# Six changes of queue order in a two-block fp32 transformer kernel: taps, key stacks, rotation tables, modulated tiles, key weights, and one root in SBUF

## The chip, the core and the metric

The kernel runs on one core of a Trainium2 chip. The metric is the device time in microseconds (us) of one execution; the median of several runs counts. The core has a matrix engine (PE), a vector engine (DVE), a scalar engine (ACT), a general engine (POOL, called G in the code), and SP, whose queue here issues the DMAs. Each engine works through its own queue in the order in which the program holds it; engines wait for one another by semaphores.

## The reference

Two transformer blocks are computed one after the other on 512 tokens of width 1024, all in fp32, batch 1. Cut to what matters:

```python
def first_block(x, ...):
    h = rms_norm(x, norm1_g)
    proj = h @ w_in                      # q, keys and values, u_conv, gates
    y_attn = nsa_attention(...) @ w_attn_br
    y_conv = conformer_conv(u_conv, ...) @ ...   # depthwise conv, 31 taps, 512 channels
    g_a, g_b = split(sigmoid(g_merge))
    x = x + (g_a * y_attn + g_b * y_conv) @ w_out
    x = x + conv_ffn(rms_norm(x, norm2_g), ffn_w_up, ..., ffn_w_down)
    return rms_norm(x, final_g)

def second_block(x, c, ...):
    # twice: h = rms_norm(x) * (1 + scale(c)) + shift(c); x = x + gate(c) * mixer(h)
    # mixer 1: dense attention with rotated q and k, and latent attention
    # mixer 2: windowed attention with sinks
    return rms_norm(x, final_norm)
```

## The kernel before

Activations lie transposed: eight tiles X[0] to X[7] (in the trace `x`) hold 128 features each by 512 tokens. A matrix product `gemm` sums over eight 128-feature tiles, and every fp32 operand is split in a high and a low part, so that one product is three PE matmuls (`mm3`: low times high, high times low, high times high; L133 to L135). A product of one 128x512 output tile over eight tiles is 24 matmuls.

A weight passes through `wload` (L101 to L114): SP issues a DMA into a raw buffer (`t` or `wr`), ACT copies the high part (L112, `wh`), and POOL or DVE subtracts to get the low part (L113, `wl`). Tiles `m`, `h`, `z` are the same parts where a weight goes to another pool. A raw buffer is free for the next DMA once the subtraction has read it; the buffers of a pool are used in turn. Which engine subtracts, and which raw pool is used, alternates by `wpools`. The order in which the four engines take their work comes from a scheduler that lays the program out ahead of time, from the order of the code and from `tc.issue_after`, which keeps an instruction from being placed ahead of a named one. Nothing is reordered at run time.

Output tiles collect in PSUM banks. Products with `wide_bank` go round the banks `pg` and `ps`, four in all; the next product in a bank waits until the engine that reads the last one (the eviction) is done.

The places that the change touches, in order of time:

- `stack_k` (L291) copies a key tile into 64-row halves: two ACT copies (L297, L299) and two DVE instructions. Four calls for the block keys `KB` stand ahead of the loop over `natural` (L478), whose four products are evicted by ACT (L488).
- `gates` makes the merge gates, each a product of 24 matmuls. The taps of convolution channel tile 0 are one ACT multiplication (L520) and one POOL addition (L521) each; those that are left over when the attention is done (`rest`, 16) are spread over the gates of the first call.
- The feed-forward down product runs in three passes. The last 128-feature tiles of weights are taken in two halves of 256 tokens by `by_halves`: eight output tiles for the first half, then eight for the second. After each half the sum of squares gives a norm: `newton` computes the inverse root by eleven small DVE instructions (L177 to L188) between SBUF and PSUM, `row_bcast` spreads it by PE (L204), and `modulated` makes eight normalised tiles (DVE L851, ACT L852, DVE L853). For the first half the eight tiles are made while PE works on the second. `by_halves` also serves the products `w_eo` and `w_oo`.
- After the first half of the down product the weights `w_kv` and `w_qa` are loaded. Then four small tables for the rotation of q and k are made by POOL (L908).
- In the `w_eo` product the squares are ACT instructions (L243, L246), summed by DVE (L254) and PE (L264). The weights `w_ok` of the keys that follow are loaded by the same `wload`.

## Time and profile before

| what | value |
|---|---|
| median of 3 runs | 1297.09 us (1296.65 to 1299.78) |
| profiled execution, its own time | 1301.25 us |
| span of the profiled execution | 1299.5 us |
| PE busy | 1251.2 us, 96% of the span |
| DVE, ACT, POOL busy | 68%, 54%, 56% |

The span is the time from the first to the last instruction of the profiled execution; what lies around it is 1.75 us here. Times in the text are microseconds from the span's start. In the rows, names are tiles of the program, `a<-b` reads "a is made from b", and `xN` is a count. The clock in the tables of stretches is the granted clock of PE as a share of full speed: 1.00 is 2.4 GHz, 0.50 is 1.2 GHz.

### The profile page before, as it was taken

The page shows a single profiled execution, that of the slowest core. Times are in us where ns is not written, and L with a number is a line of the kernel's source. Part 1 is how long each engine was busy: PE and PEld are TensorE (multiplying, and loading weights), DVE is VectorE, ACT ScalarE, POOL GpSimd, SP SyncE. Part 2 cuts the span into 40 slices and gives each one's busy share as a digit, 9 for nine tenths or more (in the row PEclk, how much of TensorE's full clock was granted, in tenths as well). Part 3 has the DMA queues.
Part 4 walks back from the last instruction along what each step waited for, and adds up shares of the span by engine and source line. Part 5 has one row for each costly group of instructions (what it writes and reads, how often), then busy time and mean ns, then how long its engine had stood idle before and what let it go on. Part 6 is the DMA issues. An engine that isn't in the chain of part 4 may idle for free. (4 is left out here: it accounts for less than half of the span.)

```text
span 1299.5 us, 19323 instructions
## 1 busy us (share of the span) xinstructions
PE 1251.2 (96%) x6369; PEld 1041.1 (80%) x6369; DVE 883.7 (68%) x2000; ACT 701.9 (54%) x1488; POOL 730.1 (56%) x718
## 2 busy tenths in 40 slices
PE   7999998999999999999999999999999989999997
PEld 6878876888888888888887798877777788888786
DVE  6756666986644878776777258576787766656565
ACT  6756777434444444423443243585766635766554
POOL 5557875773644666655665423386664423676542
PEclk9999998999999999999999999999999989999998
DMA  6221111342434555576553402111111111111221
GB/s 220 90 75 58 33 44 47 91 147 73 138 98 129 165 169 166 161 254 221 171 159 94 145 23 56 49 45 58 53 50 41 33 50 57 58 57 57 66 74 65
DMA packets 71971, 124.74 MB, mean 96 GB/s; under 512 B 8256, under 2 KB 17344, under 8 KB 71872
## 3 DMA queue, kind: packets, MB, share of 16 engines
q1 hardware_dynamic: 71872, 123.52, 30.8%
q8 instruction: 50, 0.82, 0.3%
q14 instruction: 49, 0.40, 0.1%
HBM read 121.39 MB, written 2.10 MB: 95 GB/s over the span
## 5 line engine op out<-in xcount | busy, mean ns | idle before, releaser
L113 POOL TENSOR_TENSOR wl<-wr,wh 128x512 fp32r<-128x512 f32 (+2 forms) x215 | 281.1, 1311 | 260.8 <-ACT wh L112 205.8
L133 PE MATMUL pg<-h,wl 128*128 128x512 f32 x628 | 250.2, 398 | 5.8 <-POOL wl L113 3.9
L135 PE MATMUL pg<-h,wh 128*128 128x512 f32 x628 | 248.0, 395 | 0.0
L134 PE MATMUL pg<-h,wh 128*128 128x512 f32 x628 | 247.6, 394 | 0.0
L112 ACT ACTIVATE wh<-wr 128x512 fp32r<-128x512 f32 (+2 forms) x215 | 132.6, 618 | 164.2 <-PE pg L135 77.7
L133 PEld LDWEIGHTS pg<-h,wl 128*128 128x128 f32 x628 | 119.1, 190 | 29.6 <-POOL wl L113 4.9
L135 PEld LDWEIGHTS pg<-h,wh 128*128 128x128 f32 x628 | 119.0, 189 | 23.3
L134 PEld LDWEIGHTS pg<-h,wh 128*128 128x128 f32 x628 | 119.1, 190 | 22.5 <-issue 0.7
L113 POOL TENSOR_TENSOR m<-t,m 128x512 fp32r<-128x512 f32 (+1 forms) x67 | 89.6, 1337 | 77.3 <-ACT m L112 73.4
L337 DVE TENSOR_TENSOR t<-pt,t 128x512 fp32r<-128x512 f32 (+1 forms) x160 | 97.5, 631 | 28.7 <-ACT t L336 27.4
L342 PE MATMUL po<-t,h 128*128 128x512 f32 (+3 forms) x384 | 110.7, 364 | 4.4 <-DVE t L337 1.9
L133 PE MATMUL ps<-h,wl 128*128 128x512 f32 x260 | 103.1, 396 | 3.2 <-POOL wl L113 3.2
L135 PE MATMUL ps<-h,wh 128*128 128x512 f32 x260 | 102.2, 393 | 0.0
L134 PE MATMUL ps<-h,wh 128*128 128x512 f32 x260 | 101.8, 391 | 0.0
L336 ACT ACTIVATE t<-pt 128x512 fp32r<-128x512 f32 (+1 forms) x160 | 84.3, 552 | 22.6 <-PE pt L332 21.9
L342 PEld LDWEIGHTS po<-t,h 128*128 128x128 f32 x384 | 65.7, 188 | 29.2 <-ACT t L336 13.7
L332 PE MATMUL pt<-k,p 128*128 128x128 f32 x576 | 85.3, 273 | 2.9 <-POOL p L1010 2.9
L332 PEld LDWEIGHTS pt<-k,p 128*128 128x128 f32 x576 | 69.0, 140 | 14.0 <-POOL p L1010 4.4
L1010 POOL TENSOR_SCALAR p<-p,s 128x512 f32<-128x512 f32 x64 | 45.4, 712 | 55.6 <-DVE s L1009 53.5
L778 DVE CUSTOM_DVE_ANT_0 b<-b,z 128x512 f32<-128x512 f32 x48 | 75.5, 1572 | 0.0
L112 ACT ACTIVATE m<-t 128x512 fp32r<-128x512 f32 (+2 forms) x76 | 46.2, 608 | 31.0 <-PE ps L133 9.4
L133 PEld LDWEIGHTS ps<-h,wl 128*128 128x128 f32 x260 | 49.1, 189 | 14.9 <-POOL wl L113 4.8
(441 smaller groups left out, 3046.1 us busy)
## 6 DMA issues: line engine op xcount, KB each, us to landing
b<-ada_t SPq DMA_DIRECT2D x48, 256.0 KB, 3.1
z<-ada_t SPq DMA_DIRECT2D x48, 256.0 KB, 3.2
t<-w_up SPq DMA_DIRECT2D x44, 256.0 KB, 2.9
wr<-w_up SPq DMA_DIRECT2D x44, 256.0 KB, 2.8
wr<-w_g SPq DMA_DIRECT2D x32, 256.0 KB, 2.9
t<-w_dn SPq DMA_DIRECT2D x23, 256.0 KB, 2.7
wr<-w_br SPq DMA_DIRECT2D x16, 256.0 KB, 2.6
wr<-w_gt SPq DMA_DIRECT2D x16, 256.0 KB, 2.9
```

The costliest lines, as they stand in the source:

```text
L112: A.activation(hi[:, :z], raw[:, :z], AF.Copy)
L113: eng.tensor_sub(lo[:, :z], raw[:, :z], f(hi[:, :z]))
L133: PE.matmul(ps, ll, rh, start=start and i == 0, stop=False)
L134: PE.matmul(ps, lh, rl, start=False, stop=False)
L135: PE.matmul(ps, lh, rh, start=False, stop=stop and i == n - 1)
L332: PE.transpose(ps[:, o:o + 128], src, ident)
L336: evac[:] = [A.activation(hi[:, :n], ps[:, :n], AF.Copy)]
L337: evac.append(V.tensor_sub(lo[:, :n], ps[:, :n], f(hi[:, :n])))
L342: PE.matmul(o[:, a:b], v, t[:, pa:pa + b - a], start=start and z == 0, stop=stop and z == 1)
L778: V.tensor_tensor_reduce(out=raw, in0=raw, in1=CA[z], op0=OP.mult, op1=OP.add, scale=1.0, scalar=0.0, accum_out=MA[l][:, z, m:m + 1])
L1010: scaled[0] = G.tensor_scalar(p, p, sm[:, 1:2], 0.0, op0=OP.mult, op1=OP.add)
```

## The change

Six edits. (A) The 16 left-over taps of tile 0 begin with the third gate: none in the first two, 16 over the other 12. (B) The key stacks move into the loop over `natural`, after its second and fourth product. (C) The rotation tables are kept behind the last POOL subtraction of a weight that stood in the program when the first half of the down product ended (`halved`). (D) The modulated tiles of the first half no longer stand ahead of the second half's evictions: each follows the eviction of the same number (`then`), in the down product and in `w_eo`. (E) The key weights `w_ok` are kept behind the last square of the first half of `w_eo`. (F) The two roots of `w_oo` use `newton_alone`: eight instructions, all in SBUF.

```diff
+        sub = eng.tensor_sub(lo[:, :z], raw[:, :z], f(hi[:, :z]))
+        if eng is G:
+            halved[:] = [sub]
...
+    def newton_alone(x):
+        n = x.shape[1]
+        y, t = [new("s", (128, 20))[:, :n] for _ in range(2)]
+        V.tensor_scalar(y.bitcast(I32), x.bitcast(I32), -0.5, float(0x5F3759DF), op0=OP.mult, op1=OP.add)
+        V.tensor_mul(t, y, y)
+        V.scalar_tensor_tensor(t, t, -0.5 * 0.375, x, op0=OP.mult, op1=OP.mult)
+        V.scalar_tensor_tensor(y, t, 1.5 * 0.375, y, op0=OP.add, op1=OP.mult)
+        V.tensor_mul(t, y, y)
+        V.scalar_tensor_tensor(t, t, 64.0 / 9, x, op0=OP.mult, op1=OP.mult)
+        V.scalar_tensor_tensor(t, t, -10.0 / 3, t, op0=OP.add, op1=OP.mult)
+        root[:] = [V.scalar_tensor_tensor(y, t, 5.0, y, op0=OP.add, op1=OP.mult)]
+        return y
...
-    for t in tkb:
-        KB.append([stack_k(t, 0), stack_k(t, 64)])
...
+        if i % 2:
+            KB.append([stack_k(tkb[i // 2], 0), stack_k(tkb[i // 2], 64)])
...
-            for t in rest[len(rest) * i // len(todo):len(rest) * (i + 1) // len(todo)]:
+            j, k = max(i - 2, 0), len(todo) - 2
+            for t in rest[len(rest) * j // k:len(rest) * (j + 1) // k] if i > 1 else ():
                 conv_tap(0, t)
...
-    def by_halves(src, k0, k1, xs, evac, raw, ws):
+    def by_halves(src, k0, k1, xs, evac, raw, ws, then=[]):
...
                     with after_root():
                         evac(th, m, ps[:, 0:256], c)
+                    if m < len(then):
+                        then[m]()
...
-        for k in range(KT):
-            modulated(k, fgn[:, k:k + 1], md[:, k:k + 1], R[:, 256:512], c)
+        then[:] = [lambda k=k, R=R, c=c: modulated(k, fgn[:, k:k + 1], md[:, k:k + 1], R[:, 256:512], c)
+                   for k in range(KT)]
+        for step in then if th else ():
+            step()
         xr.append((r0, c))
         if th == 0:
+            tables_after = halved[0]
...
+            with tc.issue_after(getattr(tables_after, "ins", tables_after)):
+                G.tensor_tensor(t, cc(tname).rearrange("p (i d) -> p i d", d=64),
+                                row[:, go:go + 64].unsqueeze(1).to_broadcast([128, 4, 64]), op=OP.mult)
...
+        if th == 0:
+            first_squared = squared[0]
...
-        ps = gemm(I["w_ok"][m], H)
+        with tc.issue_after(getattr(first_squared, "ins", first_squared)):
+            ps = gemm(I["w_ok"][m], H)
...
-        R = row_bcast(rsqrt(sums[th].sums("po"), 1.0 / D, EPS), "pt")
+        R = row_bcast(rsqrt(sums[th].sums("po"), 1.0 / D, EPS, alone=True), "pt")
```

How the instructions stand on the engines shows more than the diff. Line numbers of the changed kernel are higher by 1 to 32 (L113 is L114 there, L521 is L539, L246 is L264, L851 is L873, L908 is L935, L1156 is L1183).

POOL at the first merge gates, before: `h_1077` is the sum of the taps, and `wl_2808` and `wl_2814` are the two low weights of the second gate.

```order
L614 TENSOR_SCALAR p_2586<-p_2586,s_2618,k_521 128x512
L521 TENSOR_TENSOR h_1077<-h_1077,r_2661 128x512
L521 TENSOR_TENSOR h_1077<-h_1077,t_2803 128x512
L113 TENSOR_TENSOR wl_2808<-wr_2806,wh_2807 128x512
L113 TENSOR_TENSOR wl_2814<-wr_2812,wh_2813 128x512
L521 TENSOR_TENSOR h_1077<-h_1077,t_2851 128x512
```

The same in the changed kernel; the second gate's lows are now `wl_2805` and `wl_2811`, and the third gate's are `wl_2850` and `wl_2856`.

```order
L114 TENSOR_TENSOR wl_2766<-wr_2764,wh_2765 128x512
L114 TENSOR_TENSOR wl_2805<-wr_2803,wh_2804 128x512
L114 TENSOR_TENSOR wl_2811<-wr_2809,wh_2810 128x512
...
L632 TENSOR_SCALAR p_2586<-p_2586,s_2618,k_497 128x512
L539 TENSOR_TENSOR h_1077<-h_1077,r_2661 128x512
L114 TENSOR_TENSOR wl_2850<-wr_2848,wh_2849 128x512
L114 TENSOR_TENSOR wl_2856<-wr_2854,wh_2855 128x512
```

The second gate's lows moved from behind the first left-over tap to right behind the first gate's, 33 rows earlier in the queue.

POOL in the second pass of the down product, before: `wl_7376` to `wl_7470` are the low weights of its last four output tiles.

```order
L113 TENSOR_TENSOR wl_7347<-wr_7345,wh_7346 128x384
L113 TENSOR_TENSOR h_7665<-t_7663,h_7664 128x512
L113 TENSOR_TENSOR wl_7376<-t_7374,wh_7375 128x512
L113 TENSOR_TENSOR wl_7382<-wr_7380,wh_7381 128x384
L113 TENSOR_TENSOR wl_7411<-t_7409,wh_7410 128x512
L113 TENSOR_TENSOR wl_7417<-wr_7415,wh_7416 128x384
L113 TENSOR_TENSOR wl_7464<-wr_7462,wh_7463 128x512
L113 TENSOR_TENSOR wl_7470<-t_7468,wh_7469 128x384
```

The same in the changed kernel; `b` are the rotation tables, `h_7745` and `h_7757` low parts of `w_qa`.

```order
L114 TENSOR_TENSOR h_7665<-t_7663,h_7664 128x512
L935 TENSOR_TENSOR b_8038<-k_8036,k_108 128x256 x2
L935 TENSOR_TENSOR b_8041<-k_8036,k_108 128x256
L114 TENSOR_TENSOR wl_7376<-t_7374,wh_7375 128x512
L935 TENSOR_TENSOR b_8041<-k_8036,k_108 128x256
L114 TENSOR_TENSOR wl_7382<-wr_7380,wh_7381 128x384
L114 TENSOR_TENSOR wl_7411<-t_7409,wh_7410 128x512
L114 TENSOR_TENSOR wl_7417<-wr_7415,wh_7416 128x384
L114 TENSOR_TENSOR wl_7464<-wr_7462,wh_7463 128x512
L114 TENSOR_TENSOR h_7745<-t_7743,h_7744 128x512
L114 TENSOR_TENSOR h_7757<-t_7755,h_7756 128x512
L114 TENSOR_TENSOR wl_7470<-t_7468,wh_7469 128x384
```

The tables left two places further ahead (before `wl_7236` and before `wl_7277`) and now stand in front of `wl_7376` and `wl_7382`; two subtractions for `w_qa` now stand in front of `wl_7470`. ACT at the same place, in the changed kernel; before, `wh_7469` came right behind `wh_7463`:

```order
L113 ACTIVATE wh_7416<-wr_7415 128x384
L113 ACTIVATE wh_7463<-wr_7462 128x512
L113 ACTIVATE h_7738<-wr_7737 128x512
L113 ACTIVATE h_7744<-t_7743 128x512
L113 ACTIVATE h_7756<-t_7755 128x512
L113 ACTIVATE wh_7469<-t_7468 128x384
```

Three copies of `w_qa` weights moved ahead of `wh_7469`; the buffer `wr_7737` that the first of them reads is one that `wl_7417` has to free before its DMA is issued.

ACT at the end of the first half of `w_eo`, before; `p_11164` and `p_11188` are the squares of the last two X tiles, and `wh` are the key weights.

```order
L246 ACTIVATE p_11141<-x_114 128x256
L112 ACTIVATE wh_11596<-wr_11595 128x512
L246 ACTIVATE p_11164<-x_115 128x256
L112 ACTIVATE wh_11639<-wr_11638 128x512
L112 ACTIVATE wh_11645<-wr_11644 128x512
L246 ACTIVATE p_11188<-x_116 128x256
```

The same in the changed kernel.

```order
L264 ACTIVATE p_11141<-x_114 128x256
L264 ACTIVATE p_11164<-x_115 128x256
L264 ACTIVATE p_11188<-x_116 128x256
L113 ACTIVATE wh_11590<-wr_11589 128x512
L113 ACTIVATE wh_11596<-wr_11595 128x512
L113 ACTIVATE wh_11639<-wr_11638 128x512
```

The squares no longer stand behind weights. A little later DVE's sixteen modulation instructions (L851, L853), which stood ahead of the third eviction of the second half (`x_111`), are mixed with the evictions, one tile of each kind at a time.

## Rows read from the trace of the kernel before

**Rows 1.** The page's first line: busy us, share of the span, instructions.

```profile
PE 1251.2 (96%) x6369; PEld 1041.1 (80%) x6369; DVE 883.7 (68%) x2000; ACT 701.9 (54%) x1488; POOL 730.1 (56%) x718
```

**Rows 2.** PE's waits: line, what ended them, us in total, times, longest.

```profile
PE pg L133 <- POOL wl L113: 3.9, 2, 3.7
PE ps L133 <- POOL wl L113: 3.2, 4, 1.5
PE po L264 <- DVE z L254: 3.0, 2, 2.8
...
PE ps L133 <- DVE x L1156: 2.0, 1, 2.0
PE pg L133 <- ACT p L488: 1.9, 1, 1.9
```

**Rows 3.** Stretches: us, busy us of five engines, PE's clock, DMA share.

```profile
217.14:223.97 6.83, 5.92 (x14) 4.68 (x15) 2.45 (x4) 2.91 (x6) 6.83 (x6) 0.50 0.41 118
226.40:253.60 27.20, 27.20 (x122) 22.52 (x121) 24.55 (x37) 12.66 (x21) 19.18 (x15) 1.00 0.33 96
...
1046.58:1049.99 3.41, 3.41 (x18) 3.41 (x18) 0.97 (x7) 0.67 (x2) 2.22 (x2) 0.50 0.59 162
...
708.90:728.50 19.60, 16.28 (x67) 12.07 (x67) 8.37 (x13) 7.22 (x14) 14.90 (x13) 1.00 0.51 150
742.20:758.00 15.80, 15.80 (x126) 15.12 (x125) 3.64 (x8) 2.93 (x7) 0.00 (x0) 1.00 0.06 17
```

**Rows 4.** Timeline of POOL at the first gates: start, us, operation, idle before.

```profile
215.10 1.66 POOL L521 TENSOR_TENSOR h<-h,t 128x512 f32<-128x512 f32 x1 [10.62 <-ACT t L520]
216.72 2.52 POOL L113 TENSOR_TENSOR wl<-wr,wh 128x512 fp32r<-128x512 f32 x2
```

**Rows 5.** Timeline of ACT at the key stacks: the last copy, the first eviction.

```profile
47.89 0.63 ACT L299 ACTIVATE h<-p 64x512 fp32r<-64x512 f32 x1
48.54 0.49 ACT L488 ACTIVATE p<-ps,s 128x280 f32<-128x280 f32 x1
```

**Rows 6.** Timeline of POOL: the first rotation table alone, the last two.

```profile
696.05 0.74 POOL L908 TENSOR_TENSOR b<-k,k 128x256 f32<-128x256 f32 x1 [0.63 <-DVE p L789]
...
709.68 2.33 POOL L908 TENSOR_TENSOR b<-k,k 128x256 f32<-128x256 f32 x2
```

**Rows 7.** Timeline of POOL, second pass of the down product.

```profile
725.20 1.29 POOL L113 TENSOR_TENSOR h<-t,h 128x512 fp32r<-128x512 f32 x1
...
733.77 2.36 POOL L113 TENSOR_TENSOR wl<-wr,wh 128x384 fp32r<-128x384 f32 x2 [3.82 <-ACT wh L112]
```

**Rows 8.** DMA issues from 726 to 737: KB each, median us to landing.

```profile
wr<-w_kv SPq DMA_DIRECT2D x2, 256.0 KB, 3.7
wr<-w_qa SPq DMA_DIRECT2D x2, 256.0 KB, 3.5
```

**Rows 9.** Timeline of DVE in the same pass.

```profile
733.31 0.69 DVE L113 TENSOR_TENSOR m<-wr,m 128x512 fp32r<-128x512 f32 x1 [8.34 <-ACT m L112]
```

**Rows 10.** Timelines of DVE and ACT, end of the first half of `w_eo`.

```profile
1042.46 0.47 DVE L1156 SCALAR_TENSOR_TENSOR x<-ps,k,x 128x256 f32<-128x256 f32 x1
...
1044.35 0.63 ACT L112 ACTIVATE wh<-wr 128x512 fp32r<-128x512 f32 x1 [2.40 <-DMA wr<-w_ok]
```

**Rows 11.** Timeline of DVE over the two roots of `w_eo`.

```profile
1048.85 0.16 DVE L198 TENSOR_SCALAR s<-po 128x2 f32<-128x2 f32 x1 [2.72 <-PE po L264]
...
1052.62 1.26 DVE L851 SCALAR_TENSOR_TENSOR p<-x,k,pt 128x256 f32<-128x256 f32 x3 [0.76 <-PE pt L204]
...
1058.86 0.48 DVE L1156 SCALAR_TENSOR_TENSOR x<-ps,k,x 128x256 f32<-128x256 f32 x1
...
1071.36 1.07 DVE L853 SCALAR_TENSOR_TENSOR h<-p,k,h 128x256 fp32r<-128x256 f32 x2
```

**Rows 12.** Timeline of DVE at the last root: its first and last instruction.

```profile
1289.57 0.16 DVE L198 TENSOR_SCALAR s<-po 128x2 f32<-128x2 f32 x1 [1.15 <-PE po L264]
...
1291.63 0.16 DVE L188 SCALAR_TENSOR_TENSOR s<-po,s 128x2 f32<-128x2 f32 x1
```

More of the change, by code (lines that the diff above doesn't have):

```diff
@@ L194, in after_root, with rsqrt @@
         return tc.issue_after(getattr(root[0], "ins", root[0]))
-    def rsqrt(src, scale, eps, bank=None):
+    def rsqrt(src, scale, eps, bank=None, alone=False):
         x = new("s", (128, 20))[:, :src.shape[1]]
         V.tensor_scalar(x, src, scale, eps, op0=OP.mult, op1=OP.add)
-        return newton(x, bank)
+        return newton_alone(x) if alone else newton(x, bank)
     def row_bcast(col, tag="ps"):
@@ L879, in build @@
     xr = []
-    for th, c in by_halves(I["w_dn"], 18, 22, ACTV[18:], down, "t", ws):
+    then = []
+    for th, c in by_halves(I["w_dn"], 18, 22, ACTV[18:], down, "t", ws, then):
         v = new("s", (128, 16))[:, 0:4]
@@ L1159, in build @@
     H = [None] * KT
-    for th, c in by_halves(I["w_eo"], 4, 8, OC[4:], attn_out, "m", ws):
+    for th, c in by_halves(I["w_eo"], 4, 8, OC[4:], attn_out, "m", ws, then):
         R = row_bcast(rsqrt(sums[th].sums("po"), 1.0 / D, EPS), "pt")
-        for k in range(KT):
-            modulated(k, MOD[1][1][:, k:k + 1], MOD[1][0][:, k:k + 1], R[:, 0:256], c)
+        if th == 0:
+            first_squared = squared[0]
+        then[:] = [lambda k=k, R=R, c=c: modulated(k, MOD[1][1][:, k:k + 1], MOD[1][0][:, k:k + 1], R[:, 0:256], c)
+                   for k in range(KT)]
+        for step in then if th else ():
+            step()
     md = MOD[1][0]
```

8 lines of the change are left out of this document (4 added, 4 removed).

## The prediction

> **What bounds the kernel now.** I read the page's first line first, then PE's waits, then the granted clock by stretches, and last the timelines of the engines that end those waits. PE is busy for 96% of the span [rows 1], so the kernel can gain only where PE waits, or where it works at half clock; nothing else in the change has a price. The waits that the change aims at are five [rows 2]: 3.7 us for one POOL low weight at the merge gates, 3.2 us in four waits for lows in the down product, 2.8 us for a sum of squares `z`, 2.0 us for an eviction L1156, 1.9 us for an eviction L488. Some of them are followed by a stretch at a granted clock of 0.50, which is 1.2 of 2.4 GHz [rows 3]: 6.83 us after the 3.7 us wait, and 3.41 us after the 2.8 us wait (the row at 1046.58; two more of this length, at 49.89 and 1060.23, follow the waits of 1.9 and 2.0). Work at half clock takes twice as long, so these cost 5.92 / 2 = 3.0 us and 3.41 / 2 = 1.7 us. The waits in the down product lie in a stretch at 1.00 throughout [rows 3] (the row from 708.90): there only the waiting counts.
>
> Unit times: five gates of 24 matmuls take 27.20 us [rows 3], so a 512-wide matmul is 0.227 us and a gate 5.44; the 256-wide one of the halves is 0.12 (15.80 us by 126 records, the small sums among them).
>
> **A, taps.** POOL waits 10.62 us for the scaled input of a left-over tap, adds it, and only then makes the second gate's lows at 216.72 [rows 4]. In the changed order these lows stand right behind the first gate's, far ahead, and no tap stands before them. The wait (3.7) and the stretch at half clock (3.0) go: 6.7. The two subtractions (2.52) now come earlier on POOL among the attention's instructions, which may cost something there, and 16 taps in 12 gates mean two in some gates: 2.52 + 2 x 1.3 = 5.1 us of POOL against 5.44 of PE, which still fits. DVE, at 24.55 of 27.20 us in the gates [rows 3], has no part in these taps. I take 6.5, range 5 to 6.7.
>
> **B, key stacks.** Eight copies of some 0.63 stand on ACT ahead of the first L488 (48.54) [rows 5], and PE's bank waits for that eviction. Without them it runs when its product is done, and PE's 1.9 and the 1.7 of half clock go: 3.6. The copies (8 x 0.65 = 5.2 us of ACT) then stand between the later evictions, four behind the second and four behind the fourth; the third may be late. I take 3.2, range 2.2 to 3.6.
>
> **C, rotation tables, and what moves with them.** I walk this stage on the clock of before. With two tables fewer ahead of `wl_7236` and two ahead of `wl_7277`, the chain of buffer, DMA, ACT and POOL runs 0.9 to 1.2 us earlier; `wl_7347` (725.24) and `h_7665` (ends 726.49, [rows 7]) come 1.1 earlier, so POOL is at the tables at 725.4.
> Three tables now stand ahead of `wl_7376`. A table took 0.74 with DVE idle and 2.33 / 2 = 1.17 beside DVE [rows 6]. DVE is idle here, for 8.34 us up to 733.31 [rows 9], so I take 0.74: `wl_7376` (1.29) ends at 725.4 + 2.2 + 1.3 = 728.9. PE has nine matmuls from 724.1 on and wants it at 726.2: a wait of 2.7 that was not there. The page "SBUF — State Buffer" of the Trainium skill ("Who interferes with whom") says that a DVE instruction with two SBUF inputs and a POOL instruction exclude each other; the two prices in the rows agree with it, and by it the low price holds while DVE idles.
> Then the fourth table and `wl_7382` (1.0) end at 730.6. Only then is the next `wr` buffer issued; it lands 3.7 later [rows 8], at 734.3; ACT's 0.6 and 0.5 (a copy is 0.63 for 512 columns, [rows 10], less for 384) and POOL's 1.0 give `wl_7417` at 736.4. PE, from 728.9 with 33 matmuls (7.5), arrives at 736.4: just in time.
> Now the second new wait. ACT holds `h_7738` ahead of `wh_7469`, and its buffer is issued when `wl_7417` is done: 736.4 + 3.5 [rows 8] = 739.9. Three copies and `wh_7469` end at 742.2. POOL starts `h_7745` when the second copy is done, 741.0, and `h_7757` behind it: 743.6; `wl_7470` ends at 744.6. PE wants it 21 matmuls after `wl_7417`, at 736.4 + 4.8 = 741.2: it waits 3.4 us. Before, `wl_7470` was done at 733.77 + 2.36 + 1.0 = 737.1 [rows 7], and PE passed here without waiting, nine matmuls ahead of the halves at 742.2 [rows 3], at 740.2. So the stage ends 744.6 - 740.2 = 4.4 us later than before, its gains included.
> Behind that wait DVE has weights of `w_qa` ahead of the evictions `x_115` and `x_116`, three DMAs one after the other; by the same landings the last eviction ends near 748.6, and PE's fourth half product wants that bank near 749.5: covered, by 0.9 us. Queued behind these are the squares; they start at 749. I take C as a loss of 4.4. It is 3.5 if landings are a little quicker; with tables at 1.17 it is 5.7; and a stretch at half clock behind the second wait adds 1.7: to 7.4.
>
> **E, key weights.** The last squares of the first half wait on ACT behind `wh`, which waits 2.40 for its DMA [rows 10]; PE waits 2.8 for the sum. Without it the square of `x_115` runs when its eviction is done (1042.46 + 0.47 = 1042.9, [rows 10]), the sum is ready about 1043.2 where PE arrives at 1042.9, and the root starts (L198) at 1045.1 instead of 1048.85 [rows 11], since the 1.7 of half clock goes too. Gain 3.7. If DVE's evictions stay as late as they are, 0.6 of the wait is left and perhaps half clock: range 2.3 to 3.8.
>
> **D, modulated tiles.** In the down product the one wait for an eviction was 0.3: gain 0.3. In `w_eo` the sixteen modulation instructions (from 1052.62) delay `x_111` to 1058.86 [rows 11]; interleaved, the evictions keep ahead of PE, and 2.0 + 1.7 would go. But not all of it is kept. The work of DVE is the same, some 0.4 us an instruction and four instructions a product, 1.57 us against PE's 12 x 0.12 = 1.44, so DVE stays the slower one. And in the new PE order the sums for the second root stand behind 25 matmuls and not 15, and have 16 matmuls behind them to cover the root, and not 25. Counted from the first root's broadcast on: the sums end at +12.9 (before +14.5); the root takes 2.7 and now three other DVE instructions (1.1 in all, before one); broadcast and the first modulated tile take 2.4; PE goes on at +18.8. Before, that tile was done at 1071.36 + 0.5 = 1071.9 [rows 11], +19.9. So 1.1 is left of 3.7, and two new waits of about 1.6 and 1.8 us stand around the broadcast, which may bring half clock (1.7). Both places: gain 1.4, range -0.5 to 3.
>
> **F, last root.** From the first to the last instruction of the root 1291.63 - 1289.57 = 2.06 us go by in steps of 0.2 [rows 12]; the new one has three instructions fewer, two of which were on the path and one half beside another: 1.6, gain 0.5. The first root of `w_oo` lies beside PE's work. The page "Perfetto Trace Analysis" of the Trainium skill ("Optimizing Scalar/DVE Operations") puts DVE's access at 125 ns for PSUM and 60 for SBUF; by it eight instructions in SBUF would gain another 0.5 (an estimate from that page). The rows give 0.16 to 0.17 us for either kind, so I leave that out.
>
> **Sum.** -6.5 - 3.2 + 4.4 - 3.7 - 1.4 - 0.5 = -10.9 against the profiled execution's own 1301.25 us (span 1299.5 and 1.75 around it): 1290.4. That execution is 4.2 above the median of 1297.09; a difference of waits does not depend on that, so I put it on the median: 1286.2. About 0.3% (3.9 us) is what a measurement of this kernel can tell from no change.
>
> **Rivals.**
> 1. The new waits in C do not form: low weights and DMAs find slack that I do not see, and only the gain of 1.1 is left. For it: POOL idles 3.82 us ahead of 733.77 [rows 7], room for tables. Against: that room is behind the lows which wait, the order is fixed, and a buffer can't be issued before it is read. C is then -1.1, the sum -16.4: 1280.7.
> 2. Half clock comes back: behind both waits of C, and around the second root of `w_eo`. For it: the waits there (2.7, 3.4, 1.8) are as long as those that were followed by 0.50 (1.9 to 3.7). Against: half clock ahead of the second wait of C is hidden in it. Two more stretches, +3.4, with slow tables +1.3: 1290.9.
> 3. A is partly lost: the second gate's lows still come late, because their DMAs or ACT copies do, and a wait of 1.5 with half clock for 3.41 us stays: +3.2, 1289.4.
> 4. Slower: after the two waits of C the clock stays at 0.50 through the halves. Each us of full-speed work there then costs one more; the halves are 33 us of it. Without it the change gains 10.9, so it is slower by 0.3% from 14.8 us of such work on, a stretch of 29.6 us; at 33 the time is 1319. For it: the halves hold PE on short matmuls and sums. Against: the longest stretch after a wait was 6.83 us, and the halves of before ran at 1.00 [rows 3].
> 5. The change does not do what it says for the tables: by the order they do stand ahead of three lows of the running pass, and C above is built on that.
>
> **How the numbers follow.** Forecast 1286.2: chance 0.58, own range 1282 to 1290. Rival 1: 0.17. Rival 2: 0.13. Rival 3: 0.08. Rival 4: 0.03, and 0.01 for others. The range takes in most of rivals 1 to 3 and the bounds of C: 1280 to 1293. Faster than 1293.2 by these cases: 0.88; within 0.3%: 0.08, the far ends of rivals 2 and 3; slower: 0.04.
>
> **What would show it.** A: no wait of PE for lows at 214, and clock 1.00 there. B: none for L488. C: PE's waits for POOL lows grow from 3.2 to about 6 us, one ended by the low behind the tables, one by the last low of the pass (`wl_7470`). E: `z` wait under 0.6. D: no wait for L1156, but new ones at the broadcast (L221) and the first modulated tile. F: root 1.6 us. The forecast is wrong if the waits in C are under 2 us in sum, or if new stretches at 0.50 outnumber the one left at the end.

## The result, and the profile after

| kernel | median of its runs | against the kernel before, same chip and hour |
|---|---|---|
| before | 1298.43 us (1296.65 to 1301.12, 4 runs) | |
| changed | 1288.64 us (1287.92 to 1290.61, 4 runs) | 0.9927, 95% interval 0.9910 to 0.9943 |

The change saves 9.8 us, in the range and near the 10.9 us of the prediction's sum. The profiled execution took 1287.92 us, with a span of 1285.9. That is 13.3 us less than the profiled execution of before (13.6 between the spans); the 3.5 us beyond the medians are scatter of executions: the profiled one of before lay above all its timed runs, the one of after is the fastest of its own. So single parts are compared below by their places in the trace, and the whole by medians.

The first line of the page of after (it answers [rows 1]): PE has the same 6369 instructions and is busy 7.9 us less.

```profile
PE 1243.3 (97%) x6369; PEld 1035.6 (81%) x6369; DVE 884.6 (69%) x1994; ACT 701.9 (55%) x1488; POOL 729.2 (57%) x718
```

PE executes the same matmuls, so what it is busy less is work that no longer runs at half clock; its other gain is waiting. (The first stretch at half clock, at the start of the execution, is part of that: it ended at 12.34 us before and at 9.60 after.) PE's waits in the changed kernel (what waited, what ended it, us in total, times, longest; they answer [rows 2]):

```profile
PE pg L136 <- POOL wl L114: 4.1, 3, 2.6
...
PE pt L221 <- DVE s L183: 1.8, 1, 1.8
PE ps L136 <- DVE h L875: 1.8, 1, 1.8
...
PE pt L221 <- DVE s L205: 1.2, 1, 1.2
PE po L282 <- DVE z L272: 1.1, 2, 0.9
...
PE ps L136 <- POOL wl L114: 0.9, 2, 0.5
```

Three of the five waits of before are gone: 3.7 at the gates, 1.9 for L488, 2.0 for L1156. The `z` wait has shrunk from 2.8 to 0.9. The low weights of the down product cost more than before: 4.1 + 0.9 = 5.0 us, against 3.3 (the 3.2, and 0.16 that the row of 3.9 holds beside the 3.7 at the gates [rows 2]). Of the 5.0, two waits make 3.9 (PE's timeline; the second is the one for `wl_7470`):

```profile
715.52 0.50 PE L136 MATMUL pg<-h,wl 128*128 128x512 f32 x1 [2.64 <-POOL wl L114]
...
730.94 0.50 PE L136 MATMUL pg<-h,wl 128*128 128x512 f32 x1 [1.29 <-POOL wl L114]
```

The small ones that are left have shrunk from 3.3 to 1.1. Besides, two waits are new, L221 for the second root of `w_eo` (the 1.2) and the first modulated tile behind it (1.8, L875).

Stretches of the changed kernel (us, busy us of PE, PE's weight loads, DVE, ACT and POOL, PE's clock, DMA share, GB/s; they answer [rows 3]):

```profile
217.14:223.97 6.83, 6.83 (x31) 5.65 (x31) 6.04 (x11) 3.47 (x6) 4.95 (x5) 1.00 0.35 96
...
716.16:719.57 3.41, 3.41 (x10) 2.64 (x9) 0.00 (x0) 0.00 (x0) 2.19 (x2) 0.50 0.50 154
742.20:758.00 15.80, 15.80 (x130) 15.34 (x130) 7.73 (x28) 6.38 (x15) 2.56 (x2) 1.00 0.06 15
1057.49:1060.90 3.41, 3.14 (x14) 3.14 (x15) 3.41 (x10) 1.69 (x4) 0.00 (x0) 0.50 0.00 0
```

The stretch at 217, at half clock before, is now at 1.00. (Its place in the program now comes some ten us earlier; no stretch at 0.50 lies between 9.60 and 716.) The halves (742 to 758) stay at 1.00. Two new stretches at 0.50 stand behind the new waits: at 716 behind the tables, at 1057 behind the second root of `w_eo`.

By position of the same PE instruction in both traces, the 13.6 us between the spans are made up so: 4.0 by the key stacks and the start (60.50 against 56.50); 6.8 by the gates (310.68 against 299.92, less the 4.0); 1.5 by a stretch of half clock at 313 that before had and after did not, a matter of the execution; minus 2.8 in the down product (833.45 against 823.93); 0.1 up to 1034; 3.5 in the `w_eo` product (from 1034.08 and 1024.50 to 1289.53 and 1276.49); 0.5 at the last root (its wait is 1.82 where it was 2.31).

### The profile page after: what moved, and what is told of

It is laid out like the page before. It is cut to its first block, busy times and chain, and to the rows that moved or that the text cites. A ratio compares the mean times of both kernels' runs of the same rounds, so it can differ in the third digit from the quotient of the medians.

```text
span 1285.9 us, 19309 instructions
## 1 busy us (share of the span) xinstructions
PE 1243.3 (97%) x6369; PEld 1035.6 (81%) x6369; DVE 884.6 (69%) x1994; ACT 701.9 (55%) x1488; POOL 729.2 (57%) x718
## 5 line engine op out<-in xcount | busy, mean ns | idle before, releaser
L114 POOL TENSOR_TENSOR wl<-wr,wh 128x512 fp32r<-128x512 f32 (+2 forms) x215 | 281.2, 1313 | 264.1 <-ACT wh L113 209.2
L113 ACT ACTIVATE wh<-wr 128x512 fp32r<-128x512 f32 (+2 forms) x215 | 131.7, 617 | 149.0 <-PE pg L138 78.3
L114 POOL TENSOR_TENSOR m<-t,m 128x512 fp32r<-128x512 f32 (+1 forms) x67 | 89.6, 1337 | 69.3 <-ACT m L113 63.8
L360 PEld LDWEIGHTS po<-t,h 128*128 128x128 f32 x384 | 65.7, 188 | 29.2 <-ACT t L354 13.6
L113 ACT ACTIVATE m<-t 128x512 fp32r<-128x512 f32 (+2 forms) x76 | 46.2, 608 | 29.8 <-PE ps L136 11.3
L544 DVE SCALAR_TENSOR_TENSOR pt<-z,k,pt 128x512 f32<-128x512 f32 x87 | 58.5, 748 | 0.0
```

Source lines behind the costliest of these rows:

```text
L113: A.activation(hi[:, :z], raw[:, :z], AF.Copy)
L114: sub = eng.tensor_sub(lo[:, :z], raw[:, :z], f(hi[:, :z]))
L360: PE.matmul(o[:, a:b], v, t[:, pa:pa + b - a], start=start and z == 0, stop=stop and z == 1)
L544: return V.scalar_tensor_tensor(conv[c], zs[c][:, t:t + 512], cv("cw", c * 31 + t), y, op0=OP.mult, op1=OP.add)
```

## The experiments

Times of a kernel are medians; before had 1297.5 to 1298.5 us beside them. Executions of one kernel scatter by some 2 us either way, at most by 5 (before had 1293.75 to 1303.90). A part of it is that a stretch of half clock of 3.41 us, worth 1.7, follows the waits of 0.5 us at 300 and 0.9 us at 1034 in some traces and not in others. Where an edit is worth less than that, its own stage in the trace decides. There is one trace of each kernel. For the down product I give the length of a stage that holds nothing else of the change: from the end of PE's wait for a square near 388 us to the start of its wait near 824 us. It is 432.8 us before and 435.7 us after. The runs below without A, without B, without E, without F and without D in `w_eo` have the down product of the changed kernel, so they show how far this stage scatters: 435.6, 437.0, 439.1, 435.7 and 435.6. The 439.1 holds one stretch of half clock more than the others, at 390.

### The down product: which of the two edits brings which wait

**Without C.** The rotation tables stand where they did; D is kept.

```diff
-            with tc.issue_after(getattr(tables_after, "ins", tables_after)):
-                G.tensor_tensor(t, ...)
+            G.tensor_tensor(t, ...)
```

> The changed kernel without edit C: the rotation tables are free again and stand on POOL ahead of wl_7236 and wl_7277, as in the kernel before; the query weights still stand ahead of wh_7469. Changed kernel: PE waits 0.5, 0.4 and 2.6 us for lows in the second pass, 3.41 us at half clock (1.7 lost) and 1.3 us for wl_7470, some 6.5 us in all. My theory (two new waits, each with a cause of its own): no wait of 2.6 and no half clock, but the waits of before come back (0.8, 0.3, 0.6, 1.5) and the one for wl_7470 grows to about 2.8, since half clock no longer hides a part of it: 6.1 in all, the time within 1 us of the changed kernel. Rival (the tables are the whole loss of this stage): the wait for wl_7470 is under 1 us and the time 2.5 to 3 us shorter than the changed kernel's.

Measured: 1290.67 us (1288.4 to 1293.2), 0.9944 [0.9924, 0.9963]. The stage is 437.0 us, 1.3 more than in the trace of the changed kernel; the scatter is as large. PE's waits for low weights in it:

```profile
PE pg L136 <- POOL wl L114: 3.1, 2, 2.9
PE ps L136 <- POOL wl L114: 3.0, 4, 1.5
```

The four small waits of before are back (0.8, 0.2, 0.5 and 1.5), and the wait of 2.9 us for `wl_7470`, which I had put down to C, is there without C. POOL's timeline shows it as in the changed kernel, two `w_qa` lows `h` ahead of it (start, us, instruction):

```profile
726.57 2.52 POOL L114 TENSOR_TENSOR h<-t,h 128x512 fp32r<-128x512 f32 x2 [3.12 <-ACT h L113]
729.04 1.44 POOL L114 TENSOR_TENSOR wl<-t,wh 128x384 fp32r<-128x384 f32 x1
```

So the tables are not what brings `w_qa` ahead of the last low.

**Without D in the down product.** The modulated tiles of the first half are made in one block again; C is kept.

```diff
-    for th, c in by_halves(I["w_dn"], 18, 22, ACTV[18:], down, "t", ws, then):
+    for th, c in by_halves(I["w_dn"], 18, 22, ACTV[18:], down, "t", ws):
...
-        then[:] = [lambda k=k, R=R, c=c: modulated(...) for k in range(KT)]
-        for step in then if th else ():
-            step()
+        for k in range(KT):
+            modulated(k, fgn[:, k:k + 1], md[:, k:k + 1], R[:, 256:512], c)
```

> The changed kernel without edit D in the down product (kept in w_eo): the modulated tiles stand ahead of the second half's evictions again, and by the order the query weights no longer stand ahead of wh_7469. My theory: the wait for wl_7470 (1.3 us) is gone, the wait of 2.6 us behind the tables and 3.41 us of half clock stay, and a wait of 0.3 for an eviction of the second half comes back: about 1 us shorter than the changed kernel. Rival (the wait for wl_7470 follows from the late tables alone): it stays at 1 us or more, and the time is the changed kernel's or 0.3 us longer.

Measured: 1287.69 us (1286.15 to 1289.1), 0.9922 [0.9902, 0.9942]; the stage is 434.75, 1.0 less than in the changed kernel. PE's waits in it:

```profile
PE pg L136 <- POOL wl L114: 2.4, 2, 2.2
...
PE ps L136 <- POOL wl L114: 1.6, 2, 1.2
```

The 2.2 is the wait behind the tables; at `wl_7470` PE does not wait at all. On ACT, `wh_7469` (the first row) comes ahead of `w_qa` again:

```profile
722.73 0.53 ACT L113 ACTIVATE wh<-t 128x384 fp32r<-128x384 f32 x1 [0.68 <-POOL wl L114]
727.59 0.63 ACT L113 ACTIVATE z<-wr 128x512 fp32r<-128x512 f32 x1 [4.33 <-DMA wr<-w_qa]
```

So D moved the `w_qa` weights: the program holds the weights' loads behind the modulated tiles in its text, and when D took those into the second half, the scheduler put three copies of `w_qa` ahead of `wh_7469`. The four combinations by stage length: neither edit 432.8, C alone 434.75 (+1.9), D alone 437.0 (+4.2), both 435.7 (+2.9). Each of the last three holds one stretch of half clock of 3.41 us. By the scatter of the stage, D alone and both are not told apart; that each edit brings its own wait is. The two losses overlap: a wait behind the tables makes PE later at `wl_7470`.

**Tables later.** The tables are held behind `wl_7470`, the last low of the pass, rather than behind the one that stood ahead of them; D is kept.

```diff
         V.tensor_add(X[m], X[m], ps)
+    tables_after = halved[0]
...
         if th == 0:
-            tables_after = halved[0]
```

> The changed kernel with the tables held behind the last low weight of the second pass (wl_7470) and not behind the last of the halves' lows that stood in the program. My theory: the 2.6 us wait shrinks to about 0.4, no half clock in the pass, the wait for wl_7470 is 1.8 us: some 3.4 us shorter than the changed kernel. Rival (the ring of raw buffers bounds the pass, tables or not): the waits in the pass still add up to over 5 us, and the time stays within 1 us.

Measured: 1289.09 us (1287.15 to 1293.86), 0.9936 [0.9915, 0.9957]: no gain in the median, where 3.4 us were expected. In the stage the mechanism is right and the size is not: 434.1 us, 1.6 less. PE's waits:

```profile
PE pg L136 <- POOL wl L114: 3.1, 3, 2.7
...
PE ps L136 <- POOL wl L114: 1.6, 2, 1.2
```

The wait behind the tables (2.6) and its half clock are gone, but now PE comes early to `wl_7470` and waits 2.7 there, not 1.3. Without D it had not waited there. The waits for lows add up to 4.7 us, just under the 5 of the rival, whose time (within 1 us of the changed kernel) came true. The 1.6 us of the stage do not show in the time; the profiled execution had more half clock outside the stage, at 303 (3.41 us, which the changed kernel's did not have) and at 1057 (6.83 us, not 3.41).

**Tables and `w_qa` later.** The same, and the splits of the `w_qa` weights are held behind `wl_7470` too. The trace shows that this holds POOL's subtractions alone: on ACT two copies of `w_qa` still end ahead of `wh_7469`, and DVE's first low of `w_qa` starts at 724.86, ahead of `wl_7470` at 725.84.

```diff
-            wqa = wsplit(I["w_qa"], KT, 512, ...)
+            with tc.issue_after(getattr(tables_after, "ins", tables_after)):
+                wqa = wsplit(I["w_qa"], KT, 512, ...)
```

> As the run before, and the query weights w_qa are held behind that same low as well. My theory: only the first two small waits of the pass (0.9 us in sum) and some 0.4 are left, none for wl_7470: some 5.2 us shorter than the changed kernel, 1283 to 1284. Rival (the weights are then late elsewhere): a new wait stands in the second half or at the first product with w_qa near 780, and no more than 3.4 us is gained.

Measured: 1291.19 us (1287.43 to 1291.76), 0.9941 [0.9922, 0.9961]: the theory's 5.2 us did not come and the rival's new wait did; the stage is 436.55, longer than in the changed kernel. The waits for lows shrink to 1.6 and 0.4, but a new one is longer than what they gave (first fence PE's waits, then DVE's and ACT's timelines):

```profile
PE po L299 <- ACT p L295: 2.6, 1, 2.6
```

```profile
732.14 0.74 DVE L114 TENSOR_TENSOR h<-wr,h 128x512 fp32r<-128x512 f32 x1 [1.75 <-ACT h L113]
732.80 0.68 DVE L847 TENSOR_TENSOR x<-x,pg 128x512 f32<-128x512 f32 x1
733.40 0.41 DVE L899 TENSOR_TENSOR x<-x,ps 128x256 f32<-128x256 f32 x1
```

```profile
732.02 0.61 ACT L113 ACTIVATE h<-t 128x512 fp32r<-128x512 f32 x1
733.85 0.42 ACT L295 ACTIVATE p<-x 128x256 f32<-128x256 f32 x1 [1.21 <-DVE x L899]
```

DVE stands idle for 1.75 us for a copy of `w_qa`, which stands on ACT behind another that waits 2.0 us for its DMA; the evictions L847 and L899 stand behind it in DVE's queue, the first square L295 behind these, and PE's sum (L299) behind the square. 6.83 us at half clock follow (734.39). The prediction had seen this queue ("DVE has weights of `w_qa` ahead of the evictions") and found it covered by 0.9 us. PE's waits in front of it were that cover; when they went, it became the bound.

**Plain tiles and tables later.** No D in the down product, and the tables held behind `wl_7470`: the edits of the second and third experiment together.

> The changed kernel with two things different in the down product: the modulated tiles of the first half in one block as before (no D there), and the four rotation tables held behind the last of GpSimd's subtractions for the down weights (wl_7470) instead of the one ahead of the tables. My theory: the tables cost 2.2 to 2.6 us at the second pass's third weight, and D in the down product lets the eight copies of the query weights go ahead of the last down weights on ScalarE, which is the 2.7 us at wl_7470 that came up when only the tables were held. Undone together neither wait is there: about 0.4 + 1.2 us of waits stay ahead of the second pass's products, against 4.8 us and a half clock of 1.7 us in the changed kernel. So 3 to 4.5 us less: 1284.1 to 1285.6 us. Rival one: the tables, now later, are late for the rotations that read them, or hold GpSimd's merging of query weights (a new wait of 1 to 3 us behind 730 us): 1287 to 1289 us. Rival two: without D the wait ahead of the halves' second products grows (0.27 us were there in the run without D): under 0.5 us.

Measured: 1285.71 us (1282.0 to 1290.14), 0.9901 [0.9877, 0.9925], 2.9 us under the changed kernel; the two intervals overlap. No low wait is left but two small ones (0.4 and 0.9), and POOL has its order back: the last low `wl`, then the four tables at 0.70 us each.

```profile
721.28 1.02 POOL L114 TENSOR_TENSOR wl<-t,wh 128x384 fp32r<-128x384 f32 x1
722.26 2.81 POOL L933 TENSOR_TENSOR b<-k,k 128x256 f32<-128x256 f32 x4
```

The median lies between two groups of executions, 1282.0 to 1283.2 and 1288.2 to 1290.1. The profiled one (1288.22) is of the second, and has this stretch in the halves:

```profile
758.38:768.62 10.24, 10.24 (x50) 10.24 (x49) 3.45 (x10) 3.69 (x9) 5.19 (x4) 0.50 0.17 42
```

PE is busy throughout at half clock, which costs 5.1 us, about as far apart as the groups (5.0 to 8.1). The last wait ahead of it is 0.26 us at 756.10. With it the stage is 435.5, without it, 435.5 - 5.1 = 430.4: the last kernel below, which has the same down product and no such stretch, shows 430.8. So with the right partner C gains 2 us on the stage of before, where the change as it stands loses 2.9, but only in executions without that stretch: with it, this stage loses 2.7. That the three longer executions are those with the stretch is likely and not shown, as one alone was profiled.

### The gates, the key stacks and the last root

**Without A.** The left-over taps go over all steps again.

```diff
-            j, k = max(i - 2, 0), len(todo) - 2
-            for t in rest[len(rest) * j // k:len(rest) * (j + 1) // k] if i > 1 else ():
+            for t in rest[len(rest) * i // len(todo):len(rest) * (i + 1) // len(todo)]:
```

> The changed kernel with the convolution's taps spread over all steps again (part A undone, all else as changed). My theory: GpSimd's subtraction for the first weight behind the taps is late again as in the trace of before, where TensorE waited 3.74 us at 214.30 and ran at half clock for 6.83 us behind it (3.4 us lost): +6.7 us on the changed kernel's 1288.6 us, 1295.3 us. Rival: part of the gain of 6.8 us that the ledger shows there came from elsewhere (the earlier start of everything by B); then a wait of 2 us or less stands there, with at most 3.4 us at half clock: +3.5 us, 1292.1 us.

Measured: 1296.69 us (1293.56 to 1298.97), 8.0 above the changed kernel; 0.9987 [0.9974, 0.9999]. The wait (with two of the down product in the same row; the longest is this one) and the stretch behind it are those of before:

```profile
PE pg L136 <- POOL wl L114: 7.7, 3, 3.7
```

```profile
213.73:220.55 6.82, 5.56 (x13) 4.40 (x14) 2.81 (x5) 3.03 (x5) 6.82 (x6) 0.50 0.38 109
```

3.7 and 5.56 / 2 = 2.8 are 6.5: the theory holds, the rival's wait of 2 us or less does not. The remaining 1.5 of the 8.0 would be explained by the half clock at 309, which the profiled execution had; of the other nine no trace tells.

**Without B.** The key stacks stand in one block again.

```diff
+    for t in tkb:
+        KB.append([stack_k(t, 0), stack_k(t, 64)])
...
-        if i % 2:
-            KB.append([stack_k(tkb[i // 2], 0), stack_k(tkb[i // 2], 64)])
```

> The changed kernel with the key stacks put back as one block ahead of the natural-order projections (part B undone, all else as changed). My theory, from the trace of before: the wait of 1.88 us at 47.69 for the first natural projection's evictions comes back, and with it the half clock of 3.413 us that followed it and costs half of that, 1.7 us. So the first 60 us are about 3.2 to 3.6 us longer than in the changed kernel, and the time is 3.4 us above its 1288.6 us: 1292. Rival: the half clock there came from the start of the execution (it ended at 12.3 us before and at 9.6 us after) and not from this wait; then only 1.9 us come back and no half-clock record stands near 50 us.

Measured: 1292.84 us (1291.3 to 1296.37), 4.2 above the changed kernel; 0.9958 [0.9943, 0.9974]. Both the wait and the half clock are back, and PE reaches the wait behind the natural projections at 59.93, not at 56.50: 3.4 us later.

```profile
PE pg L136 <- ACT p L507: 1.9, 1, 1.9
```

```profile
49.74:53.15 3.41, 3.41 (x9) 2.65 (x8) 1.40 (x6) 1.88 (x7) 0.00 (x0) 0.50 0.02 5
```

**Without F.** The last roots use the PSUM form again.

```diff
-        R = row_bcast(rsqrt(sums[th].sums("po"), 1.0 / D, EPS, alone=True), "pt")
+        R = row_bcast(rsqrt(sums[th].sums("po"), 1.0 / D, EPS), "pt")
```

> The changed kernel with the last two roots on the PSUM columns again (part F undone, all else as changed). My theory: the wait ahead of the last broadcast is 2.31 us again instead of 1.82, and the end is 0.5 us later; that is less than five rounds tell apart from the changed kernel, so the wait in the trace decides: 1289.1 us. Rival: the wait is set by the sums ahead of it and not by the root's eight or ten operations: 1.8 us stay.

Measured: 1288.35 us (1287.84 to 1289.07), which does not differ from the changed kernel; 0.9919 [0.9903, 0.9935]. The wait at the last broadcast is 2.31 us (the longest of this row) and not 1.82, as expected:

```profile
PE pt L221 <- DVE s L205: 4.5, 3, 2.3
```

So the root's length sets that wait, but half a microsecond is not visible in the time.

### The `w_eo` product

**Without E.** The key weights `w_ok` are not held behind the last square of the first half.

```diff
-        with tc.issue_after(getattr(first_squared, "ins", first_squared)):
-            ps = gemm(I["w_ok"][m], H)
+        ps = gemm(I["w_ok"][m], H)
```

> The changed kernel without part E (the key weights' product of the last stage may stand ahead of the first half's squares again; the modulated tiles still go behind the second half's evictions). My theory: the wait of 2.8 us for the sums of squares (it was 2.82 us ahead of the product of ones in the trace of before, and is 0.94 us in the changed kernel) comes back, with a half clock of 3.413 us that costs 1.7 us: +3.6 us, 1292.2 us. Rival: with the tiles moved too, the two parts hide one another: the wait is only 1 to 1.5 us and no half clock follows, and E alone was worth under 1 us: 1289.3 us.

Measured: 1294.0 us (1290.76 to 1298.52), 5.4 above the changed kernel; 0.9959 [0.9942, 0.9976]. PE's wait, ACT's cause and the stretch behind it:

```profile
PE po L282 <- DVE z L272: 2.8, 2, 2.6
```

```profile
1038.98 0.63 ACT L113 ACTIVATE wh<-wr 128x512 fp32r<-128x512 f32 x1 [2.20 <-DMA wr<-w_ok]
1039.52 0.40 ACT L264 ACTIVATE p<-x 128x256 f32<-128x256 f32 x1
```

```profile
1041.91:1048.73 6.82, 6.82 (x35) 6.82 (x34) 2.82 (x15) 0.80 (x2) 1.52 (x2) 0.50 0.38 118
```

A square again stands 2.2 us behind a weight's DMA. The rival falls: D doesn't hide this. The half clock was 6.8 us here and not 3.4. That would make E worth 5.3 and not 3.6, near the 5.4 of the medians; but this profiled execution was the slowest of its eleven, and how much half clock the others had no trace tells.

**Without D in `w_eo`.** The modulated tiles in one block behind the first root; D is kept in the down product.

```diff
-    for th, c in by_halves(I["w_eo"], 4, 8, OC[4:], attn_out, "m", ws, then):
+    for th, c in by_halves(I["w_eo"], 4, 8, OC[4:], attn_out, "m", ws):
```

> The changed kernel without part D in the last attention's output product (all eight modulated tiles of the first half in one block behind the first root; D in the down product stays). My theory: the wait of 2.0 us ahead of the second half's first products comes back at about 1047 us with a half clock of 3.413 us behind it, and the two waits round the second root (1.24 and 1.75 us in the changed kernel, with a half clock behind them) shrink to the 0.8 us that the trace of before has there, without a half clock. Waits 2.0 + 0.8 against 3.0, one half clock against one: the time is within 1 us of the changed kernel, 1288.4 us. Rival: D is worth here the 1.1 us or more that I gave it (the second root's waits stay at 3 us whatever the tiles' order is, since the root is a chain of small operations on VectorE): then 2 us and a half clock are added, +2 to +3.7 us, 1290.6 to 1292.3 us.

Measured: 1290.96 us (1290.45 to 1291.87), 2.3 above the changed kernel; 0.9941 [0.9928, 0.9955]. PE's waits around the second half:

```profile
PE ps L136 <- DVE x L1183: 2.5, 1, 2.5
...
PE ps L136 <- DVE h L875: 0.8, 1, 0.8
```

They are the two that the theory named (it had 2.0 for the first), 2.5 + 0.8 with one half clock, against 1.2 + 1.8 with one half clock; the rival's 3 us at the second root are not there, though the median lies in its range. From the product near 1026 to the last root the kernel takes 253.0 us, the changed one 252.0. So D is worth 1.0 here by the trace. The other 1.3 of the median would be explained by the half clock at 302 that the profiled execution had; whether the other four had it no trace tells, and it stays open whether D is worth 1.0 or 2.3 here.

### A version that beats both

The second root of `w_eo` is made on the path in the changed kernel. DVE's timeline there, towards its end, and PE's wait for it:

```profile
1054.16 0.42 DVE L324 TENSOR_TENSOR h<-ps,h 128x256 fp32r<-128x256 f32 x1 [0.25 <-ACT h L323]
1054.50 0.15 DVE L203 TENSOR_SCALAR s<-po 128x2 f32<-128x2 f32 x1
1054.56 0.41 DVE L324 TENSOR_TENSOR h<-pg,h 128x256 fp32r<-128x256 f32 x1
1054.89 0.16 DVE L204 TENSOR_TENSOR po<-po,s 128x2 f32<-128x2 f32 x1
```

```profile
1055.30 0.71 PE L221 MATMUL pt<-k,s 128*128 128x128 f32 x4 [1.24 <-DVE s L205]
```

Two low parts of values (L324) go into the middle of the root. A shorter root should help; on top of the version with plain tiles and late tables I gave both roots of `w_eo` the short form of F.

```diff
-        R = row_bcast(rsqrt(sums[th].sums("po"), 1.0 / D, EPS), "pt")
+        R = row_bcast(rsqrt(sums[th].sums("po"), 1.0 / D, EPS, alone=True), "pt")
```

> The version with plain tiles in the down product and the tables held behind wl_7470, and besides with the short root in SBUF, which the changed kernel has in the last product, for the two roots of the last attention's output product. My theory: each of the two roots has two operations less, so that the wait of 1.25 us ahead of the second broadcast becomes 0.75 us; the first root is hidden. So 0.5 us less than the version without it. What decides the median is another thing: in that version a half clock of 10.24 us at 758 us was in its profiled execution (1288.2 us), and three of its six executions took 1282 to 1283.2 us, which I read as executions without it. So 1282 to 1283 us or 1288 us, with the median anywhere between. Rival: VectorE's two evictions of 0.4 us that stood inside the second root's chain still go into it in another place, and the wait stays 1.25 us.

Measured: 1283.8 us (1282.76 to 1286.52), 0.9889 [0.987, 0.9907]. The wait of 1.25 at the second broadcast is gone, more than I expected; but PE now waits 2.48 us at the first, which had been hidden. DVE's timeline of this first root, and POOL's beside it:

```profile
1031.60 0.52 DVE L176 TENSOR_SCALAR s<-s 128x2 int32<-128x2 int32 x1
1032.15 1.21 DVE L177 TENSOR_TENSOR s<-s 128x2 f32<-128x2 f32 x1
1033.40 1.19 DVE L178 SCALAR_TENSOR_TENSOR s<-s,s 128x2 f32<-128x2 f32 x1
1034.62 0.16 DVE L179 SCALAR_TENSOR_TENSOR s<-s,s 128x2 f32<-128x2 f32 x1
```

```profile
1030.81 3.75 POOL L114 TENSOR_TENSOR wl<-wr,wh 128x512 fp32r<-128x512 f32 x3 [3.75 <-ACT wh L113]
```

The steps with all inputs in SBUF take 0.5 to 1.2 us each until POOL's three subtractions end at 1034.56, and 0.16 from there on. The long ones are as long as one subtraction (3.75 / 3 = 1.25), as if each step waited for one to end.

**The short root for the second half only.**

```diff
-    ... EPS, alone=True), "pt")
+    ... EPS, alone=th == 1), "pt")
```

> The version before this one, with the short root in SBUF for the second root of the last attention's output product only; the first is made on PSUM columns again. My theory, from the timeline of the version before: the short root's steps that have both inputs in SBUF took 0.52, 1.21 and 1.19 us, not 0.16, where GpSimd was subtracting key weights beside them, and TensorE waited 2.48 us for the first broadcast; the PSUM form of the same root took 0.17 us a step beside the same subtractions and made no one wait. The second root has no GpSimd work beside it, and there the short form took the wait of 1.25 us away. So 2.5 us go, and 1.25 do not come back: 2.3 us under that version, 1281.5 us (executions with a half clock in the down product 3 to 5 us above it). Rival: the first root's steps were slow for another reason, and the wait at the first broadcast stays above 1 us: 1283 us.

Measured: 1282.41 us (1280.1 to 1285.89), 0.9881 [0.9861, 0.99]: 15 us under before and 6.2 under the changed kernel. Neither broadcast of `w_eo` is waited for; the 1.8 of this row is the last product's:

```profile
PE ps L136 <- DVE h L876: 1.9, 1, 1.9
PE pt L221 <- DVE s L183: 1.8, 1, 1.8
```

The first root, in its PSUM form, meets the same three subtractions of POOL (from 1031.89 on) and is hardly slowed (DVE's timeline):

```profile
1032.68 0.17 DVE L194 TENSOR_SCALAR po<-s 128x2 int32<-128x2 int32 x1
1032.76 0.45 DVE L194 TENSOR_SCALAR s<-s 128x2 int32<-128x2 int32 x1
1033.24 0.17 DVE L197 TENSOR_TENSOR po<-po,s 128x2 f32<-128x2 f32 x1
```

Only the one step that lies wholly in SBUF (`s<-s`) is stretched, to 0.45. The stage from the product near 1021 to the last root is 250.9 us, 0.9 less than with both roots short and 1.2 less than with both long. The expected 2.3 us came as 1.4 in the median. In the traces the stage holds 3.41 us of half clock (1.7 us) behind the remaining wait of 1.9, where the version before had none behind its 1.4; without it the stage would be 2.6 shorter.

## Why the prediction came out right, and where it was not

- **A**, 6.5: 6.8 by position, 6.5 by the run without it. Right in both halves, wait and clock.
- **B**, 3.2: 3.4 by the run without it.
- **C, and what moves with it**, a loss of 4.4, or 4.1 with the 0.3 that D was to gain in this stage: the stage lost 2.9. Both waits formed where the walk put them, and PE's waits for lows came to 5.0 where about 6 were forecast. The first was 2.64 for 2.7, with tables at 0.70 each for 0.74. The second was 1.29 where the prediction says that "it waits 3.4 us" for `wl_7470`. Two steps of it were off. The forecast left out the half clock behind the first wait; it came, at 716 for 3.41 us, and brought PE 1.7 us later to `wl_7470`. Rival 2 had seen that such time "is hidden" in the second wait: it shortens the wait and leaves the stage as long as it was. And from the end of the first wait to the end of the second 15.4 us went by, where the walk has 15.7; the DMAs landed in 3.1 us, not 3.5 as [rows 8] had it (the DMA issues of after between 716 and 728: KB each, median us to landing):

```profile
wr<-w_qa SPq DMA_DIRECT2D x3, 256.0 KB, 3.1
```

  What made the stage itself better than forecast lies ahead of both waits and is the mis-sized term: the chain of lows was to run "0.9 to 1.2 us earlier" and ran 2.3 us earlier. The walk has `wl_7347` at 725.24 before; here it ends at 710.49, which is 722.9 when both are counted from the wait near 388 (POOL's timeline):

```profile
709.48 1.01 POOL L114 TENSOR_TENSOR wl<-wr,wh 128x384 fp32r<-128x384 f32 x1
```

  PE's small waits in this pass fell by 2.2 us and not by 1.1, so that the low behind the tables came 1.0 us earlier than the walk has it, at a wait of the same length. In the runs without B and without E half clock came behind the second wait (at 736 and 735) and not behind the first, and the second was then 2.6 and 3.0: the walk's 3.4 was near for that case. The stage of the run without B is 437.0, a loss of 4.2.
- **The name of the term** was wrong as well. I charged the second wait to C and wrote of D: "In the down product the one wait for an eviction was 0.3: gain 0.3". The runs without C and without D show that D brings it, and costs 4.2 us alone in the one trace. The order shown ahead of the prediction had both edits in it, and I did not ask which of them moved the three `w_qa` copies. Had only one of the edits been made, the forecast would have been off by that.
- **E**, 3.7: the `z` wait went from 2.82 to 0.94 and its half clock from 3.41 to none: 1.9 + 1.7 = 3.6. The wait itself was to be under 0.6; it is 0.94, because DVE's evictions set the last squares (on ACT the one at 1033.40 waits 1.03 us for its eviction).
- **D in `w_eo`**, 1.1: 3.5 for the stage less 3.6 for E leaves nothing; against the run without it, 1.0. The two new waits were sized at 1.6 and 1.8 and measured at 1.24 and 1.75. The forecast named half clock behind them as possible and did not count it; it came (1057, 3.41 us).
- **F**, 0.5: 0.49 in the wait.

The forecast's sum was 10.9 and the medians give 9.8. The stage of C came 1.2 us better than predicted, through the earlier chain; `w_eo` (D and E) came 1.3 worse, through half clock that no wait hid. These nearly cancel, so the total was nearer than its terms, and that is luck. By the parts of the two traces, without the half clock at 313, the gain would be 12.1; the 2.3 us between this and the medians are scatter that no trace of single executions divides up. The forecast's miss of 2.4 us is 1.1 of the sum and 1.3 of its base: the kernel before had a median of 1298.43 beside the changed kernel, and 1297.09 in the runs that I had. Of the rivals, number 2 was half right: half clock did come, behind one of C's two waits and at the second root of `w_eo`. Rivals 1 and 3 did not occur: C's waits formed, and PE does not wait at the gates. Nor did rival 4: the halves are at 1.00 in the row from 742.20. Of the signs that the forecast was wrong, one did come: the two new stretches at 0.50 (716 and 1057) outnumber the one at the end. The time stayed in the range all the same, since the one at 716 was hidden in the second wait and cost the stage nothing, and the one at 1057 cost 1.7. The sign was badly chosen: it counts stretches without asking whether a wait behind them takes them up.

## What to carry to other kernels

When a change makes several moves through one scheduler, let the order be printed for each move alone; the wait that you find may belong to another move than the one you blame. A wait that is taken away uncovers the next queue behind it, so a later place is better only if what stands behind in the same queues (here evictions behind weights on DVE) has been counted to be in time. Put half clock behind a wait into the range of a forecast and not into its sum: behind waits of 2.5 to 2.9 us these runs had from none to 6.83 us of it. Where a second wait follows that something else than PE ends, half clock ahead of it costs little or nothing, as at 716.

## What the runs showed of the hardware

- A small root step on DVE with its inputs in SBUF took 0.16 us, and up to 1.21 us while POOL subtracted 128x512 tiles in SBUF; with one input in PSUM it took 0.17 us beside the same subtractions. The page "SBUF — State Buffer" of the Trainium skill ("Who interferes with whom") says that a DVE instruction with two SBUF inputs contends with a POOL instruction that reads SBUF, and that one with at most one SBUF input, outside the two-port modes, does not; these rows agree with it. The step `s<-s` with one input (a `tensor_scalar`), 0.45 and 0.52 us where 0.16 is usual, is slowed too. The same section counts `tensor_scalar` among the operations that can enter a two-port mode and then contend; whether this step was in one no run here shows. So in these traces the root in SBUF was the shorter one only where POOL rested.
- How much half clock follows a wait is not fixed by its length. Behind waits of 2.5 to 2.9 us stood 3.41 us (without C), 6.83 us (tables and `w_qa` later) and none (both roots short, and tables later at `wl_7470`); the same 0.26 us at 756 was followed by 10.24 us at 758 in one version, and at 757 by none in another with the same down product. Differences under 2 us between medians of such kernels are therefore not to be read as an edit's worth.
